# Activation stores in larger pieces and a new order on the DMA queues: two PEER layers on one Trainium2 core

## The chip, the cores and the metric

The kernel runs on one core of a Trainium2 chip. The metric is the device time of one execution in microseconds (us). A core has five engines with an instruction stream each: TensorE (PE; its weight loads are shown as PEld), VectorE (DVE), ScalarE (ACT), GpSimd (POOL) and SyncE (SP). SP computes nothing here; it issues nearly all DMA transfers, one after the other, in the order in which they stand in its stream. POOL issues the indirect transfers (gathers). All transfers are carried out by the same 16 DMA engines.

## The reference: what is computed

The input is 256 tokens of width 1024. Two layers follow each other: an attention mixer (latent attention in layer 0, sparse attention with top-64 key selection in layer 1), each followed by a layer norm, a PEER mixer and another layer norm. The change lies in the PEER mixer, which both layers have:

```
q = (xt @ w_q).reshape(T, PEER_HEADS, 2, PEER_QDIM // 2)
s1, s2 = q[:, :, 0] · sub_keys[0], q[:, :, 1] · sub_keys[1]      # 128 keys each
v1, i1 = top_k(s1, 16);  v2, i2 = top_k(s2, 16)
best, pos = top_k(v1[..., :, None] + v2[..., None, :], 16)       # of 256 pairs
expert = (i1 * 128 + i2)[pos];  gate = softmax(best)
a  = einsum('td,ted->te', x, w_down[expert])                     # T x (8 heads x 16)
y  = einsum('te,ted->td', gelu(a) * gate, w_up[expert])
```

There are 16384 experts. Each token uses 128 of them.

## The kernel before, in words

**PEER as dense work.** Instead of gathering 128 rows per token from `w_down`, the kernel multiplies all 16384 rows with all 256 tokens. The experts stand in 128 blocks of 128. In the down stage (`for b0 in range(0, NKEYS, 2)`, L1573), a step takes two blocks: each is loaded from HBM as a 128x1024 tile `raw` (512 KB, SP, L212), split into a high and a low 16-bit half (`hi` on ACT at L152, `lo` on DVE at L161), and multiplied in 24 matmuls of 128x256 (`d`, `proj`). The result goes through Gelu on ACT (L1584 or L1586) into `A`, an array of 128 blocks x 256 tokens in on-chip memory, and is multiplied there by the gates (DVE, L1418 and L1587). The gates come as one-hot products `G` on PE, in groups of four tokens (`place`, L1400): 64 groups in all, up to two in each step of the second half of the down stage, so tokens get final in their order, and the last four are final only after the last group.

**The up stage.** `A` is then multiplied by `w_up`. The first 20 expert blocks (DENSE = 20) are used as they are: their `raw` tiles are again loaded by SP at L212. For the other 108 blocks only experts that some token uses are wanted. So their rows of `w_up` are copied, HBM to HBM, into a table (`table<-in_up`, L217, 512 KB each), the activations of `A` are stored behind them in the same table rows (`table<-arena`, L1542), and POOL gathers rows of the table, weights and activations together, by a list that DVE computes at that time (`lists`, L1421). The up stage runs over 124 items (`ITEMS`): 20 dense ones first, then the gathered ones. An item for all tokens is 12 matmuls of 128x512 (`y`). Dense items take their left operand from `A` in pairs (`cut`, L1553: `xh` on ACT, `xl` on DVE; the first pair in a spare buffer).

**What sets the order.** `Stream` (L164 on) hands blocks out. When block i is taken, blocks up to i + 3 are split (AHEAD) and blocks up to five further are loaded (DMA_AHEAD); a block's number in the stream is part of its name (`raw172`). There are six `raw` buffers, so the load of block n waits until DVE has made `lo` of block n - 6. The copies of `w_up` rows are tied to loads by `copies(li)` (L411): a table of stream positions; behind the load at such a position up to two copies are issued. In layer 0 the blocks of the down stage are 39 to 166, the dense up blocks 167 to 186, the first gathered item 187.

The stores are issued by `store(part, upto)` (L1534): one store moves four blocks of `A` for the tokens of one part, so that each of its 512 rows is as long as the part has tokens. `PARTS` (L74) cuts the tokens at 128, 192 and 224: four parts, 27 stores each in a layer. In a step of the down stage each part whose tokens are final is offered up to two stores (part 0) or three (others), L1599 to L1603. The rest follow in the first items of the up stage (L1657 to L1659). At item 12 (HEAD - 8) all stores must have been issued, and the look-ahead is raised to eight, which brings the first gathers.

The instructions of an engine run strictly in the order of its stream. That order is not that of the program text: a scheduler that models times lays it out, so a changed transfer can move ACT or DVE instructions far from it.

The lines that matter most around the stores:

```
PARTS = (0, 128), (128, 192), (192, 224), (224, 256)
...
                    if 4 * groups >= upto:
                        for _ in range(2 if part == 0 else 3):
                            store(part, b0)
```

Of the kernel before, what the change touches and what calls it, by code (L numbers as in the profile page):

```python
# [68 lines left out]
DENSE, HEAD = 20, 20  # L69
RARE = P - DENSE  # L70
JB, JO, TB, ROWTAIL = 32, 24, 16, 32
BOTHS = JB + TB
WIDE = D + T
PARTS = (0, 128), (128, 192), (192, 224), (224, 256)  # L74
FETCHED, DEEP = 9, 8
LISTED = BOTHS + 2 * JO
END = 6
# [257 lines left out]
def tile_trunk(ctx: ExitStack, tc: tile.TileContext, ins, out: bass.AP, short, shared):  # L335
# [75 lines left out]
    def copies(li):  # L411

        down = len(ws.blocks) - NKEYS
        first, few = ((12, 24), (down - 44, 46))[li]
        for n in range(RARE + 1):
            i = first + (down - first) * n // few if n < few else down + 108 * (n - few) // (RARE + 1 - few)
            ws.copied.setdefault(i, []).append((table[li][n * P : (n + 1) * P, :D], ins["up"][li][(DENSE + n) % NKEYS]))

    def add_up(li):
# [13 lines left out]
    ws = Stream(nc, raws, rings, half, split, spare16)  # L433
# [758 lines left out]
    def peer(li):  # L1192
        last = li == DEPTH - 1
# [337 lines left out]

        stored = [DENSE] * len(PARTS)

        def store(part, upto):  # L1534
# [3 lines left out]
            if b0 < b1 <= upto:  # L1538
                ts = slice(*PARTS[part])
                cols = slice(D + ts.start, D + ts.stop)  # L1540
# [32 lines left out]
        for b0 in range(0, NKEYS, 2):  # L1573
            p = ps(f"d{b0}")
            pv = p.rearrange("p (j t) -> p j t", t=T)
            chosen = ready
            for j in range(2):
                proj(pv[:, j, :], ws.get())
                ready = ready or spend(PACE)
            if b0 == 0:  # L1580
                chains["pe"] = None
            t0 = 4 * groups
            if t0 < T:
                nc.scalar.activation(A[:, b0 : b0 + 2, t0:], pv[:, :, t0:], AF.Gelu, scale=1.0 / unit)  # L1584
            if t0 > 0:
                nc.scalar.activation(pv[:, :, :t0], pv[:, :, :t0], AF.Gelu, scale=1.0 / unit)  # L1586
                dve(lambda: nc.vector.tensor_tensor(A[:, b0 : b0 + 2, :t0], A[:, b0 : b0 + 2, :t0], pv[:, :, :t0],  # L1587
                                                    op=ALU.mult))
            while groups < prepared:
                place(groups, b0 + 2)  # L1590
                groups += 1
            if chosen:
                left = max(1, (NKEYS - (END if short else 4) - b0) // 2)
                want = min(64 - groups, -(-(64 - groups) // left))
                assert want <= 3, b0
                for _ in range(min(want, 1 + groups)):
                    prepare(prepared, nc.gpsimd if want == 1 else nc.vector)
                    prepared += 1
            if short:  # L1599
                for part, (_, upto) in enumerate(PARTS):  # L1600
                    if 4 * groups >= upto:
                        for _ in range(2 if part == 0 else 3):
                            store(part, b0)  # L1603
                if groups == 64:
                    if listing[0] is None:
                        chains["dve"] = None
                        cut(0)
                        listing[0] = lists()
                    if b0 < NKEYS - 2:
                        list_on(3)  # L1610
# [34 lines left out]
        if short:  # L1645
            for i, (_, _, tiles) in enumerate(ITEMS):
                if i + 2 in PAIRED:
                    cut(PAIRED.index(i + 2))
                if i < len(ITEMS) - STAGGER:
                    blk = ws.get()  # L1650
                    rows(y4, activations(i), blk, i == 0, False, tiles)
                list_on(1)
                if i == TAIL_READY:
                    assert next(listing[0], 0) == 0
                    chains.pop("dve")
                    chains.pop("pe")
                if i < HEAD - 8:  # L1657
                    for part in range(len(PARTS)):
                        store(part, NKEYS)  # L1659
                    store(part, NKEYS)  # L1660
                if i == HEAD - 8:
                    assert stored == [NKEYS] * len(PARTS) and not ws.due, stored
                    ws.pieces = 2
                    ws.DMA_AHEAD = DEEP
                if i == len(ITEMS) - 9:
                    ws.pieces = 1
                    ws.DMA_AHEAD = Stream.DMA_AHEAD
                if i == len(ITEMS) // 2:
                    middle_loads()
            items = [(activations(i), ITEMS[i][2]) for i in range(len(ITEMS) - STAGGER, len(ITEMS))]  # L1670
        else:
            for k in range(NKEYS - STAGGER):
                rows(y4, operand(k), ws.get(), k == 0, False)
                if k == 64:
                    middle_loads()
            items = [(operand(k), (0, 1)) for k in range(NKEYS - STAGGER, NKEYS)]
# [9 lines left out]
    for c in range(0, NC, 4):  # L1686
        last = nc.sync.dma_start(xt[:, c : c + 4, :], ins["xT"][c // 4])
# [154 lines left out]
```

## Time and profile before

| | |
|---|---|
| median of 3 runs | 1579.84 us (1578.42 to 1582.33) |
| the profiled execution | 1576.3 us, its span 1574.4 us |
| PE busy | 1544.1 us, 98% of the span |
| DVE, ACT, POOL busy | 1362.9, 1081.9, 386.0 us |
| DMA | 491.11 MB, 312 GB/s on average |
| `table<-in_up` copies | 218 of 512 KB |
| `table<-arena` stores | 54 of 256 KB, 56 of 128 KB, 108 of 64 KB |

Reading it: times inside the profile count from the start of the span. Matmuls are pipelined, so the rows show how long one takes from its start to its end, while the next may begin earlier; work per time is read from starts (the chain of waits gives such pieces). The view by windows gives, for stretches of the span, the busy time of PE, PEld, DVE, ACT and POOL in this order with instruction counts, then the granted PE clock, the DMA engines' busy share and the GB/s moved. A row of the timeline gives start, duration, engine, line, operation and tile, and in square brackets how long the engine had been idle and what ended that. "SPq" is SP's queue: an issue of a DMA, which includes waits for the transfer's preconditions.

### The profile page before, as it was taken

To read this page: it belongs to the slowest core of one execution; us is meant where nothing else is said; L and a number is where in the kernel's file an instruction comes from. 1 tells how busy PE (TensorE), PEld (TensorE's weight loads), DVE (VectorE), ACT (ScalarE), POOL (GpSimd) and SP (SyncE) were. 2 spreads that over 40 slices of the span, in tenths; PEclk is the share of its full clock that TensorE was granted. 3 is DMA by queue.
4 is the path that set the end of the run, shared out by engine and by line. 5 is a ranking of instruction groups with operands and counts; after the bars stand their busy time and mean duration, and the time that the engine had idled before them with its cause. 6 is when DMAs were issued, how large, how long until landed. Compare 5 with 4: busy or idle time off the path is not lost.

```text
span 1574.4 us, 33700 instructions
## 1 busy us (share of the span) xinstructions
PE 1544.1 (98%) x12275; PEld 1136.9 (72%) x12275; DVE 1362.9 (87%) x3823; ACT 1081.9 (69%) x1968; POOL 386.0 (25%) x330
## 2 busy tenths in 40 slices
PE   9999999999999999999999999999999999999996
PEld 7769888899999444444578598878899996444443
DVE  8689999999998779788788789989999996798886
ACT  7766566698887457676577766655988884567763
POOL 2002244300000046554022111344000000366550
PEclk9999999999999999999999999999999999999998
DMA  9898899998989999998499978889878899899992
GB/s 367 333 332 322 308 335 355 368 334 301 301 284 235 238 396 346 360 370 326 166 418 378 366 289 285 317 285 319 318 272 277 290 248 215 323 319 370 388 334 88
DMA packets 235760, 491.11 MB, mean 312 GB/s; under 512 B 99904, under 2 KB 128832, under 8 KB 235584
## 3 DMA queue, kind: packets, MB, share of 16 engines
q1 hardware_dynamic: 206496, 358.31, 65.7%
q0 software_dynamic: 28800, 130.04, 22.1%
q8 instruction: 98, 1.61, 0.4%
q14 instruction: 78, 0.64, 0.1%
q10 hardware_dynamic: 288, 0.52, 0.1%
HBM read 456.03 MB, written 147.06 MB: 383 GB/s over the span
## 4 chain that ended last, share of the span: by engine, by line
PE 82%; DVE 9%; DMA 3%; issue 2%; ACT 2%; SPq 1%; POOL 0%; DVEq 0%; POOLq 0%; ACTq 0%
PE y L477 32%; PE d L477 30%; PE pq L477 4%; DVE lo L161 4%; PE G L477 4%; PE q L477 3%; DMA raw<-in_down 2%; PE v L477 2%; PE seen L477 2%; ACT hi L152 1%; SPq L1542 1%; PE qw L477 1%; PE ps L477 1%; PE h L477 1%; DVE arena L1311 1%
## 5 line engine op out<-in xcount | busy, mean ns | idle before, releaser
L477 PE MATMUL d<-xh,lo 128*128 128x256 f16 x2048 | 558.3, 273 | 3.6 <-DVE lo L161 3.4
L477 PE MATMUL d<-xh,hi 128*128 128x256 f16 x2048 | 558.2, 273 | 1.8 <-ACT hi L152 1.8
L477 PE MATMUL d<-xl,hi 128*128 128x256 f16 x2048 | 558.2, 273 | 0.0
L477 PEld LDWEIGHTS <-hi 128*128 128x128 f16 x5016 | 488.5, 98 | 59.3 <-ACT hi L152 2.1
L161 DVE SCALAR_TENSOR_TENSOR lo<-raw,hi 128x1024 f16<-128x1024 f32 (+1 forms) x363 | 455.0, 1261 | 52.4 <-ACT hi L152 49.7
L152 ACT ACTIVATE hi<-raw 128x1024 f16<-128x1024 f32 (+1 forms) x355 | 368.1, 1048 | 171.5 <-PE d L477 63.5
L208 POOL DMA_INDIRECT arena<-table,up_at x160 | 174.9, 1093 | 668.6 <-DMA raw<-in_up 511.0
L477 PEld LDWEIGHTS <-xh 128*128 128x128 f16 x1712 | 166.6, 98 | 199.0 <-ACT xh L152 3.0
L161 DVE SCALAR_TENSOR_TENSOR lo<-arena,hi 128x512 f16<-128x512 f32 (+1 forms) x382 | 259.2, 715 | 45.2 <-ACT hi L152 44.5
L477 PEld LDWEIGHTS <-lo 128*128 128x128 f16 x2508 | 245.7, 98 | 35.2 <-DVE lo L161 6.3
L477 PE MATMUL y<-hi,xl 128*128 128x512 f16 x784 | 236.5, 380 | 6.6 <-DVE xl L161 6.6
L477 PE MATMUL y<-lo,xh 128*128 128x512 f16 x784 | 236.5, 380 | 0.0
L477 PE MATMUL y<-hi,xh 128*128 128x512 f16 x784 | 236.1, 380 | 0.0
L152 ACT ACTIVATE hi<-arena 128x1024 f16<-128x1024 f32 x200 | 209.1, 1052 | 14.3 <-PE y L477 3.9
L1397 ACT ACTIVATE gate<-hot,rest 128x128 f16<-128x128 f16 x512 | 168.5, 406 | 15.9 <-DVE hot L1389 14.0
L152 ACT ACTIVATE xh<-arena 128x256 f16<-128x256 f32 (+1 forms) x214 | 86.7, 407 | 116.8 <-PE y L477 74.9
L477 PEld LDWEIGHTS <-xl 128*128 128x128 f16 x856 | 83.6, 98 | 108.4 <-DVE xl L161 8.7
L262 POOL TENSOR_TENSOR lo<-raw,hi 128x1024 f16<-128x1024 f32 x26 | 58.9, 2264 | 193.0 <-ACT hi L260 138.8
L1389 DVE TENSOR_TENSOR hot<-iota,place 128x1024 f16<-128x1024 f16 x128 | 88.0, 689 | 15.7 <-PE G L477 15.4
L161 DVE SCALAR_TENSOR_TENSOR xl<-arena,xh 128x256 f16<-128x256 f32 (+2 forms) x216 | 89.8, 419 | 8.7 <-ACT xh L152 8.3
L477 PE MATMUL G<-gate,hot 128*128 128x128 f16 x1024 | 92.3, 219 | 1.3 <-DVE arena L1418 1.0
L1307 POOL TENSOR_TENSOR arena<-arena 128x800 f32<-128x800 f16 x32 | 73.3, 2290 | 73.1 <-DVE arena L1304 62.6
(270 smaller groups left out, 1862.1 us busy)
## 6 DMA issues: line engine op xcount, KB each, us to landing
raw<-in_down SPq DMA_DIRECT2D x256, 512.0 KB
table<-in_up SPq DMA_DIRECT2D x218, 512.0 KB
raw<-in_up SPq DMA_DIRECT2D x40, 512.0 KB
table<-arena SPq DMA_DIRECT2D x54, 256.0 KB
raw<-in_peer_q SPq DMA_DIRECT2D x24, 512.0 KB
raw<-in_dsa_qk SPq DMA_DIRECT2D x16, 512.0 KB
table<-arena SPq DMA_DIRECT2D x56, 128.0 KB
table<-arena SPq DMA_DIRECT2D x108, 64.0 KB
```

Of the source, the lines that this page charges most:

```text
L152: return nc.scalar.copy(o, src) if unit == 1.0 else nc.scalar.mul(o, src, unit)
L161: return nc.vector.scalar_tensor_tensor(o, src, unit, hi, op0=ALU.mult, op1=ALU.subtract, accum_out=total)
L208: self.fetched = self.nc.gpsimd.indirect_dma_start(t, None, table, bass.IndirectOffsetOnAxis(ap=at, axis=0)).ins
L262: nc.gpsimd.tensor_tensor(lo, raw, hi if short else hi.bitcast(F32), op=ALU.subtract)
L477: return pe(lambda: nc.tensor.matmul(o, l, r, start=start, stop=stop, skip_group_check=True))
L1307: nc.gpsimd.tensor_tensor(o.rearrange("p k c -> p c k"), same, cell[t][:, h, :, None].to_broadcast([P, CELLS, TOPK]), op=ALU.mult)
L1311: dve(lambda: nc.vector.tensor_reduce(exp_[t][:, h - 1, :], held, axis=AX.X, op=ALU.add))
L1389: nc.vector.tensor_tensor(hot, iota4[:, None].to_broadcast([P, 2, P, 4]), place16[:, :, None, four].to_broadcast([P, 2, P, 4]), op=ALU.is_ ...
L1397: nc.scalar.mul(gate[:, 1, j, :], hot[:, 1, :, j], rest[:, t : t + 1])
L1542: nc.sync.dma_start(rows_of, A[:, b0:b1, ts])
```

## The change

Five things are edited, in both layers alike.

1. `PARTS` has three parts; the last is tokens 192 to 255. Its 27 stores of 128 KB replace 54 of 64 KB.
2. Part 1 is now offered two stores in a step (three before), the last part three.
3. The stores of the up stage may run to item 13, and the first gather is requested two items later (HEAD - 6 in place of HEAD - 8).
4. From item 6 until then, the look-ahead of loads is three blocks in place of five.
5. `copies` spreads the 109 copies of a layer over three stretches of stream positions. Layer 0: 32 before the down stage (24 before), 38 over its first 64 loads, 39 over the next 36. Layer 1: 46 before it (as before), 32 over its first 64 loads, 31 over the next 36. Before, the rest (85 and 63) were spread evenly over the first 108 loads.

```diff
-PARTS = (0, 128), (128, 192), (192, 224), (224, 256)
+PARTS = (0, 128), (128, 192), (192, 256)
...
-        first, few = ((12, 24), (down - 44, 46))[li]
-        for n in range(RARE + 1):
-            i = first + (down - first) * n // few if n < few else down + 108 * (n - few) // (RARE + 1 - few)
+        spans = (12, down, 32) if li == 0 else (down - 44, down, 46), (down, down + 64, 38 - 6 * li), (down + 64, down + 100, 0)
+        at = [first + (last - first) * n // many for first, last, many in spans[:2] for n in range(many)]
+        first, last, _ = spans[2]
+        left = RARE + 1 - len(at)
+        at += [first + (last - first) * n // left for n in range(left)]
+        for n, i in enumerate(at):
             ws.copied.setdefault(i, []).append((table[li][n * P : (n + 1) * P, :D], ins["up"][li][(DENSE + n) % NKEYS]))
...
-                        for _ in range(2 if part == 0 else 3):
+                        for _ in range(3 if part == len(PARTS) - 1 else 2):
                             store(part, b0)
...
-                if i < HEAD - 8:
+                if i == HEAD - 14:
+                    ws.DMA_AHEAD = Stream.DMA_AHEAD - 2
+                if i < HEAD - 6:
                     for part in range(len(PARTS)):
                         store(part, NKEYS)
                     store(part, NKEYS)
-                if i == HEAD - 8:
+                if i == HEAD - 6:
                     assert stored == [NKEYS] * len(PARTS) and not ws.due, stored
```

What this does to the instruction streams is seen at three places. In the rows below, `raw167` to `raw178` are loads of dense up blocks of layer 0, `table0<-arena` are stores, and the last number of a store is its tokens; line numbers of the changed kernel are three higher from L420 on.

SP, from the end of the down stage into the up stage of layer 0, before:

```order
L212 DMA raw169_7455<-in_up 128x1024
L1542 DMA table0_119<-arena_65 128x4x32 x3
L212 DMA raw170_7485<-in_up 128x1024
L1542 DMA table0_119<-arena_65 128x4x32 x4
L1542 DMA table0_119<-arena_65 128x4x128
L1542 DMA table0_119<-arena_65 128x4x64
L1542 DMA table0_119<-arena_65 128x4x32 x3
L212 DMA raw171_7571<-in_up 128x1024
L1542 DMA table0_119<-arena_65 128x4x128
L1542 DMA table0_119<-arena_65 128x4x64
L1542 DMA table0_119<-arena_65 128x4x32 x10
L212 DMA raw172_7601<-in_up 128x1024
```

and now, in the same place:

```order
L212 DMA raw169_7435<-in_up 128x1024
L212 DMA raw170_7465<-in_up 128x1024
L1545 DMA table0_119<-arena_65 128x4x128
L1545 DMA table0_119<-arena_65 128x4x64
L212 DMA raw171_7549<-in_up 128x1024
L1545 DMA table0_119<-arena_65 128x4x128
L1545 DMA table0_119<-arena_65 128x4x64 x11
L212 DMA raw172_7579<-in_up 128x1024
L1545 DMA table0_119<-arena_65 128x4x64
L212 DMA raw173_7624<-in_up 128x1024
L1545 DMA table0_119<-arena_65 128x4x64 x7
L212 DMA raw174_7654<-in_up 128x1024
```

Between raw169 and raw171 stood 12 stores and now stand two; the 12 between raw171 and raw172 remain, 10 of them now of 64 tokens, which need the last group of gates.

ACT, at the first items of the up stage of layer 0 (`d126` is the last step of the down stage, `hi172` the split of the sixth dense up block), before:

```order
L1586 ACTIVATE d124_7566<-d124_7566 128x512
L152 ACTIVATE hi171_7743<-raw171_7571 128x1024
L152 ACTIVATE xh_100<-arena_65 128x512 x3
L152 ACTIVATE hi172_7768<-raw172_7601 128x1024
L1586 ACTIVATE d126_7643<-d126_7643 128x512
L152 ACTIVATE xh_100<-arena_65 128x512
```

and now:

```order
L1589 ACTIVATE d124_7544<-d124_7544 128x512
L152 ACTIVATE hi171_7717<-raw171_7549 128x1024
L152 ACTIVATE xh_100<-arena_65 128x512 x3
L1589 ACTIVATE d126_7619<-d126_7619 128x512
L152 ACTIVATE xh_100<-arena_65 128x512
L152 ACTIVATE hi172_7742<-raw172_7579 128x1024
```

The split that needs raw172 stood ahead of the Gelu of d126 and now stands behind it. Layer 1 shows the same exchange with hi469.

ACT, where the attention of layer 0 begins (`kn`, `v` are results of its projections, `hi18` and `hi19` splits of weights that are used after the attention, L821 the exponentials), before:

```order
L509 ACTIVATE arena_65<-kn2_610 128x512
L152 ACTIVATE hi18_943<-raw18_566 128x1024
L509 ACTIVATE arena_65<-kn4_631 128x512
L509 ACTIVATE arena_65<-kn6_645 128x512
L152 ACTIVATE hi19_947<-raw19_615 128x1024
L821 ACTIVATE arena_65,m_675<-arena_65,m_675 128x128
L509 ACTIVATE arena_65<-v00_701 128x512
L509 ACTIVATE arena_65<-v01_702 128x512
L821 ACTIVATE arena_65,m_677<-arena_65,m_677 128x256
```

and now:

```order
L512 ACTIVATE arena_65<-kn6_647 128x512
L512 ACTIVATE arena_65<-v00_704 128x512
L512 ACTIVATE arena_65<-v01_705 128x512
L152 ACTIVATE hi18_947<-raw18_568 128x1024
L512 ACTIVATE arena_65<-v10_706 128x512
L512 ACTIVATE arena_65<-v11_707 128x512
L824 ACTIVATE arena_65,m_678<-arena_65,m_678 128x128
L824 ACTIVATE arena_65,m_680<-arena_65,m_680 128x256
L152 ACTIVATE hi19_951<-raw19_617 128x1024
```

hi18 and hi19 have moved later, hi19 behind the first two exponentials; the copies of `v` now all stand ahead of them. PE and DVE are reordered to match in this stage, with the same instructions.

## The prediction, as put on record

> **What bounds the kernel now.** First the page's span and busy times:
>
> ```profile
> span 1574.4 us, 33700 instructions
> PE 1544.1 (98%) x12275; PEld 1136.9 (72%) x12275; DVE 1362.9 (87%) x3823; ACT 1081.9 (69%) x1968; POOL 386.0 (25%) x330
> ```
>
> PE is the bound, and the change takes no matmul away. It can only win time in which PE waits, or in which its clock is low: 30 us of the span at the very most. So the second view is the windows, cut at the stages; the columns are busy PE, PEld, DVE, ACT, POOL, then PE clock, DMA share, GB/s:
>
> ```profile
> 45.00:65.00 20.00, 19.67 (x129) 17.34 (x127) 18.05 (x83) 19.47 (x58) 0.23 (x1) 1.00 1.03 415
> 139.00:306.00 167.00, 164.88 (x1501) 146.27 (x1499) 157.06 (x465) 98.86 (x127) 60.20 (x38) 1.00 0.93 336
> 306.00:504.00 198.00, 197.49 (x2190) 181.38 (x2191) 186.69 (x340) 170.02 (x439) 0.00 (x0) 1.00 0.89 300
> 504.00:531.00 27.00, 23.30 (x194) 17.73 (x193) 14.81 (x38) 11.79 (x19) 0.00 (x0) 0.99 0.96 201
> 531.00:767.00 236.00, 236.00 (x1147) 108.33 (x1146) 196.75 (x699) 151.23 (x216) 106.70 (x101) 0.99 0.90 328
> 935.00:1056.00 121.00, 117.70 (x1072) 104.34 (x1070) 111.25 (x383) 71.58 (x91) 39.54 (x30) 1.00 0.83 291
> 1302.00:1328.00 26.00, 23.14 (x194) 17.67 (x193) 14.65 (x37) 11.96 (x18) 0.00 (x0) 1.00 0.92 199
> ```
>
> PE idles where the down stage turns into the up stage (27.00 - 23.30 = 3.70 us in layer 0, 26.00 - 23.14 = 2.86 in layer 1) and in the first half of the down stages (2.12 and 3.30). The second half (0.51 in 198 us) and the up stage (none in 236) have no idle time to win. Third, whom PE waits for:
>
> ```profile
> PE y L477 <- DVE xl L161: 6.6, 2, 3.7
> PE d L477 <- DVE lo L161: 3.4, 5, 1.0
> PE d L477 <- ACT hi L152: 1.8, 1, 1.8
> ```
>
> The two longest waits are the two turns. The chain of waits shows what stands behind that of layer 0 (start, duration, what):
>
> ```profile
> 511.20 0.60 DVE arena L1418
> ...
> 523.32 3.93 DMA raw<-in_up
> ...
> 527.35 1.06 ACT hi L152
> 528.41 0.49 ACT d L1586
> ...
> 528.92 0.69 DVE arena L1587
> 529.61 0.62 DVE xl L161 x2
> ...
> 530.28 34.66 PE y L477 x152
> ```
>
> PE did not yet need the tile raw172 that was loaded at 523.32. It needed `xl`, which DVE could not make because it stood in the Gelu product of the last step (L1587), which waited for ACT's Gelu (L1586), which stood in ACT's stream behind the split of raw172. SP's timeline says why that load was late:
>
> ```profile
> 513.97 0.45 SPq L212 DMA_DIRECT2D raw<-in_up  x1
> 514.52 8.69 SPq L1542 DMA_DIRECT2D table<-arena  x12
> 523.32 0.45 SPq L212 DMA_DIRECT2D raw<-in_up  x1
> ```
>
> Twelve stores, 8.69 us, between two loads.
>
> **The change part by part: the turn.** Layer 1's chain and PE's own rows in layer 0 give the price:
>
> ```profile
> 1320.19 3.99 DMA raw<-in_up
> ...
> 1327.22 32.98 PE y L477 x152
> ```
>
> ```profile
> 520.38 0.59 PE L477 MATMUL y<-hi,spare 128*128 128x512 f16 x2
> ...
> 530.28 1.03 PE L477 MATMUL y<-hi,xl 128*128 128x512 f16 x2 [3.70 <-DVE xl L161]
> ```
>
> The same 152 matmuls take 34.66 us behind the wait of 3.70 and 32.98 behind that of 2.86: 1.68 more. The granted clock of that window tells where:
>
> ```profile
> 530.00:550.00 20.00, 19.72 (x84) 8.67 (x85) 18.45 (x59) 7.99 (x10) 2.07 (x1) 0.91 1.00 264
> ```
>
> 0.91 against 1.00 elsewhere: 9% of 20 us is 1.8 us, the same loss. So the turns cost 3.70 + 1.68 + 2.86 = 8.24 us.
>
> Does the change remove all of it? Two things are needed. First, the Gelu of d126 must not wait for raw172: in the new ACT stream it stands ahead of it, in both layers, so the wait as it was cannot recur. What is late next is raw172 itself, the sixth dense item. An item is 12 matmuls of 32.98 / 152 = 0.217 us, 2.60 us; from 520.38, item 5 begins at 520.38 + 5 x 2.60 = 533.4. Before that come the split on ACT (1.06, in the chain) and on DVE:
>
> ```profile
> L161 DVE SCALAR_TENSOR_TENSOR lo<-raw,hi 128x1024 f16<-128x1024 f32 (+1 forms) x363 | 455.0, 1261 | 52.4 <-ACT hi L152 49.7
> ```
>
> With 1.26 for it and 3.93 for the landing, raw172 must be issued by 533.4 - 1.06 - 1.26 - 3.93 = 527.1. Now SP issues raw171 without waiting for the many stores ahead of it, so it stands ready at the next twelve. Ten of these need the last gates (L1418, done at 511.20 + 0.60 = 511.80). From there SP has 527.1 - 511.8 = 15.3 us for 12 stores, 1.27 each. What stores cost, in SP's timeline (64 tokens in both rows):
>
> ```profile
> 461.39 5.75 SPq L1542 DMA_DIRECT2D table<-arena  x10
> ...
> 468.32 7.57 SPq L1542 DMA_DIRECT2D table<-arena  x7
> ```
>
> 0.58 and, behind two loads, 1.08 us each; the twelve above 0.72. None reaches 1.27. At 0.72 raw172 is issued at 520.5, 6.6 us early, at 1.08 at 524.8. After it stand seven stores to raw174 (needed two items later) and then one to four between loads, so the slack grows by 2.60 us an item, against at most 4 x 1.08 + 0.45. I take the whole 8.24; the bounds are 8.24 and, with raw172 late after all, about half (below).
>
> **Fewer stores.** 54 issues at 0.58 to 1.08 go from SP, 31 to 58 us, all in places where PE was not waiting but for the turns; beyond them 0. The bytes stay. Offering part 1 less often happens where PE idled 0.51 us in 198: 0.
>
> **First gather two items later, look-ahead three.** SP's stream has no store behind raw178 now, so the shorter look-ahead reorders nothing that stalls SP; loads then wait for the six buffers as before. The gathers:
>
> ```profile
> 547.93 2.09 POOL L208 DMA_INDIRECT arena<-table,up_at  x1 [255.07 <-DMA raw<-in_up]
> ```
>
> ```profile
> 566.18 0.31 ACT L152 ACTIVATE xh<-arena 128x128 f16<-128x128 f32 x1 [6.12 <-DMA arena<-table,up_at]
> ```
>
> POOL has nothing else to do and waits for the last store, so its gather comes when the stores have landed, not when it was requested; with the last store issued earlier it comes earlier. ACT waited 6.12 us for its first rows, and PE idled not at all in that stage: 0, with a rival below.
>
> **The copies.** Layer 0 gets 8 more before the down stage, 8 x 0.524 MB = 4.2 MB, at the 415 GB/s of the windows 10.1 us of DMA time. Free there:
>
> ```profile
> 70.00:80.00 10.00, 10.00 (x49) 4.66 (x49) 3.07 (x7) 4.11 (x5) 0.00 (x0) 1.00 0.14 54
> ...
> 110.00:120.00 10.00, 10.00 (x94) 9.14 (x93) 9.49 (x45) 5.74 (x8) 1.70 (x1) 1.00 0.68 249
> ```
>
> 8.6 and 3.2 us, 11.8: just enough. In the first half of the down stage copies fall from 85/108 = 0.79 to 38/64 = 0.59 per load (layer 1: 0.58 to 0.50). The loads in the chain of that stage, where DVE is busy 157 of 167 us, are such:
>
> ```profile
> 245.87 4.66 DMA raw<-in_down
> ```
>
> 4.66 us against 3.93 with no copies near. A buffer's round trip shortens by less than 0.73 us, and only some of the 2.12 + 3.30 us of idle time hangs on it: between 0 and 5.4, I take 1.1 (0.8 and 0.3), close to the lower end, since DVE stays full. In the last stretch there are 39 copies for 36 loads. A step's two blocks take 48 `d` and 24 gate matmuls; 2190 / 72 = 30.4 steps in 198 us are 6.51 us each, 3.26 a block. 75 transfers of 0.524 MB in 36 x 3.26 = 117 us are 335 GB/s. The stage ran at 300, but 415 stands in the row for 45 to 65 us, with copies: hidden.
>
> **The attention of layer 0.** ACT is full there (19.47 of 20.00 us). hi18 and hi19 (1.05 each) now stand within the critical work: up to +2.1. Against that other filling work moved later and PE has 0.33 us idle by the row: down to -1. I take +0.5.
>
> Sum: -8.24 - 1.1 + 0.5 = -8.8 us. The profiled execution would take 1576.3 - 8.8 = 1567.5. It lay 3.5 below the median of the runs, so for the median 1579.84 - 8.8 = **1571.0 us**. About 0.3%, 4.7 us, is what a measurement can tell from no change.
>
> **Rivals.** *The turn moves to the next load* (0.13). If stores of 256-byte rows cost 1.5 us each, raw172 is issued at 511.8 + 12 x 1.5 = 529.8, 2.7 after 527.1; PE waits 2.7 per layer, and by layer 1's row a wait this long costs no clock. For: SP's 1.08 behind loads. Against: 0.72 in the same place. Time: 1571.0 + 5.4 = 1576.4.
>
> *Early copies delay the loads of the first 139 us* (0.08). Four of the eight fall into a stretch where DMA is full (1.03): 5 us of delay. If buffers don't hide it, 1576.0; against it, the weights loaded there are used only after the attention.
>
> *Gathers become late* (0.05; slower). If the first gather did come with its request, at item 14 (520.4 + 14 x 2.60 = 556.8), it would land 566.18 - 547.93 = 18.3 later, at 575.1, and be split by 577.4, while PE, no longer delayed, needs item 20 at 572.4: 5.0 us, and 1.7 for the clock, in each layer. 1571.0 + 13.4 = 1584.4, over the time before; it decides if POOL starts after 572.4 - 2.3 - 18.3 = 551.8. Against: POOL's wait ended with a transfer.
>
> *The last copies fill the memory* (0.02; slower). The down stage would fall behind while they run. The 300 GB/s of 306 to 504 us might be all that copies and loads get: 39.3 MB would take 131 us, 14 over 117, of which the six buffers hide nearly all. [...]
>
> **How the numbers follow.** Forecast 0.72. Its own bounds are 1571.0 - 4.3 (all idle time of the down stages) = 1566.7 and 1571.0 + 2.7 = 1573.7; the two milder rivals reach 1576.4; runs scatter by about 2. I give 1567 to 1577. Faster by over 0.3% (below 1575.1): 0.70 of the forecast, a third of the milder rivals' 0.21, 0.77 together. Within 0.3%: 0.16. Slower: 0.07, the last two rivals.
>
> **What would show it.** Right: no idle time of PE over 0.5 us where `spare` is followed by `xl` in either layer; the clock at 1.00 after it; ACT's Gelu at L1589 close behind `xh` x3; raw172's load about 520; the first gather near 540. Wrong: PE waiting for `lo` of the sixth to eighth dense block; PE idle at the first gathered item; longer stretches from 0 to 139 us or in the second half of the down stage.

## The result, and the profile after

The changed kernel takes 1565.96 us (median of six runs) against 1577.9 us (six runs of before), a ratio of 0.9928 with a 95% interval of 0.9912 to 0.9945: 9 to 14 us faster. A second set of runs of the same kernel gave 0.9924 (0.9907 to 0.9941). Executions in a slower state (at most one in a set) are left out of all ratios and ranges. The forecast was 8.8 us, counted from a median of three runs of before, 1579.84 us, and the measured time lies 1 us below its range. As a sum this looks like a small miss, but that is luck: two errors of opposite sign partly cancel. The turns, with what follows them, were taken at 8.24 us and gave about 4.1; the copies, with the attention's new order, were taken at 0.6 us and gave about 7.1.

The page of the changed kernel:

```profile
span 1566.8 us, 33568 instructions
PE 1544.2 (99%) x12275; PEld 1136.4 (73%) x12275; DVE 1360.7 (87%) x3815; ACT 1080.4 (69%) x1968; POOL 390.9 (25%) x330
```

PE's busy time is the same (1544.1 before), so by these rows the span lost 7.6 us of PE's idle time. The windows of the same stages (columns as in the prediction; the cuts move with the stages):

```profile
139.00:303.00 164.00, 163.84 (x1501) 146.51 (x1499) 153.31 (x461) 100.67 (x127) 60.38 (x38) 1.00 0.87 305
306.00:500.00 194.00, 193.52 (x2148) 177.68 (x2145) 182.96 (x334) 166.03 (x428) 0.00 (x0) 1.00 0.91 314
500.00:528.00 28.00, 28.00 (x227) 20.53 (x225) 21.83 (x60) 13.52 (x25) 0.00 (x0) 1.00 0.72 189
528.00:560.00 32.00, 32.00 (x150) 14.48 (x149) 21.78 (x64) 14.99 (x20) 12.04 (x9) 1.00 1.05 379
560.00:575.00 15.00, 13.55 (x62) 5.95 (x61) 9.05 (x34) 9.32 (x13) 2.23 (x2) 1.00 0.86 324
929.00:1050.00 121.00, 118.76 (x1080) 104.89 (x1079) 113.29 (x392) 72.27 (x94) 38.66 (x30) 1.00 0.80 279
1294.00:1322.00 28.00, 28.00 (x222) 20.35 (x220) 22.17 (x60) 13.52 (x22) 0.00 (x0) 1.00 0.74 197
1355.00:1370.00 15.00, 13.55 (x62) 5.89 (x61) 10.37 (x39) 9.01 (x14) 2.69 (x3) 1.00 0.27 94
```

Read it stage by stage. Both turns (500 to 528, 1294 to 1322) have no idle time any more: 3.70 and 2.86 us are gone, and the clock behind them is 1.00. But 45 us behind each turn there is idle time that before did not have: 15.00 - 13.55 = 1.45 us, the same in both layers. And the first half of layer 0's down stage, where 2.12 us were idle, now idles 0.16; layer 1's 2.24 where it was 3.30.

The turn went as forecast. SP's timeline: twelve stores in 6.88 us (0.57 each), then raw172's load, at 515.13.

```profile
508.15 6.88 SPq L1545 DMA_DIRECT2D table<-arena  x12
515.13 0.65 SPq L212 DMA_DIRECT2D raw<-in_up  x1
```

ACT's timeline there has the Gelu of the last step (L1589) ahead of the split that waits for raw172 (the `hi` with 1.13 of idle time before it):

```profile
515.69 1.74 ACT L152 ACTIVATE xh<-arena 128x512 f16<-128x512 f32 x3
517.46 0.58 ACT L1589 ACTIVATE d<-d 128x512 f32<-128x512 f32 x1
517.95 0.62 ACT L152 ACTIVATE xh<-arena 128x512 f16<-128x512 f32 x1
519.70 1.06 ACT L152 ACTIVATE hi<-raw 128x1024 f16<-128x1024 f32 x1 [1.13 <-DMA raw<-in_up]
```

POOL's first gather starts 8 us earlier than before (547.93):

```profile
539.97 1.77 POOL L208 DMA_INDIRECT arena<-table,up_at  x1 [250.23 <-DMA raw<-in_up]
```

The new wait is seen in PE's timeline, and behind it in ACT's:

```profile
566.06 0.59 PE L480 MATMUL y<-hi,xl 128*128 128x512 f16 x2
567.72 0.59 PE L480 MATMUL y<-hi,xh 128*128 128x512 f16 x2 [1.07 <-ACT hi L152]
```

```profile
561.45 1.04 ACT L152 ACTIVATE hi<-raw 128x1024 f16<-128x1024 f32 x1
563.21 0.31 ACT L152 ACTIVATE xh<-arena 128x128 f16<-128x128 f32 x1 [0.72 <-DMA arena<-table,up_at]
566.31 0.42 ACT L152 ACTIVATE xh<-arena 128x256 f16<-128x256 f32 x1 [2.79 <-PE y L480]
566.63 1.04 ACT L152 ACTIVATE hi<-raw 128x1024 f16<-128x1024 f32 x1
```

Count items from 0. The `hi` at 566.63 is hi186, for item 19, the last dense one. In ACT's stream it stands behind the `xh` of item 26. The buffer of that `xh` is the one that item 18 reads, so ACT waited 2.79 us until PE had finished item 18, made the `xh`, and only then the operand that PE needed next. PE has to stand still for 0.42 + 1.04 us here, however early the loads are. In before hi186 stood three `xh` further forward, ahead of those of items 24 to 26. ACT took its instructions in the order of its stream although a later one could run: with these `xh` moved behind it (below), hi186 is done 5 us earlier.

### The profile page after: what moved, and what is told of

Read it like the earlier page. It is cut to its first block, busy times and chain, and to the rows that moved or that the text cites. A ratio compares the mean times of both kernels' runs of the same rounds, so it can differ in the third digit from the quotient of the medians.

```text
span 1566.8 us, 33568 instructions
## 1 busy us (share of the span) xinstructions
PE 1544.2 (99%) x12275; PEld 1136.4 (73%) x12275; DVE 1360.7 (87%) x3815; ACT 1080.4 (69%) x1968; POOL 390.9 (25%) x330
## 4 chain that ended last, share of the span: by engine, by line
PE 90%; DVE 6%; issue 2%; ACT 1%; DMA 0%; POOL 0%; DVEq 0%; POOLq 0%; ACTq 0%
PE d L480 36%; PE y L480 32%; PE pq L480 4%; PE G L480 4%; DVE lo L161 3%; PE q L480 3%; PE v L480 2%; PE seen L480 2%; PE qw L480 1%; PE s L480 1%; PE ps L480 1%; PE h L480 1%; PE qi L480 1%; DVE arena L1314 1%; PE o L480 1%
## 5 line engine op out<-in xcount | busy, mean ns | idle before, releaser
L208 POOL DMA_INDIRECT arena<-table,up_at x160 | 180.9, 1131 | 655.0 <-DMA raw<-in_up 499.7
L152 ACT ACTIVATE xh<-arena 128x256 f16<-128x256 f32 (+2 forms) x214 | 85.7, 406 | 112.3 <-PE y L480 76.4
L480 PEld LDWEIGHTS <-hot 128*128 128x128 f16 x1536 | 89.1, 113 | 2.5 <-issue 1.2
```

The source lines that it names most:

```text
L152: return nc.scalar.copy(o, src) if unit == 1.0 else nc.scalar.mul(o, src, unit)
L208: self.fetched = self.nc.gpsimd.indirect_dma_start(t, None, table, bass.IndirectOffsetOnAxis(ap=at, axis=0)).ins
L480: return pe(lambda: nc.tensor.matmul(o, l, r, start=start, stop=stop, skip_group_check=True))
```

## Which part of the change gives what: four runs

Ratios are turned into us with the median of before beside them, 1577 to 1580 us; line numbers in the kernels below differ by a few.

Two theories. *A: the turns give 8 us less what item 19 takes back, and the copies give more than the forecast's 0.6 us (1.1 of gain, 0.5 of loss in the attention).* *B: the two traces are typical, the forecast's terms are about right, and the rest is scatter.*

**The changed kernel again**, nothing altered.

> The changed kernel once more, nothing altered. Between the two profiled executions the span fell by 7.6 us (1574.4 to 1566.8), but the medians of six runs fell by 11.9 us (1577.9 to 1565.96), and the profiled execution of the changed kernel was, with 1568.7, among the slowest of its six. Theory 'the trace is at the slow end of its kernel': the ratio comes out at 0.991 to 0.9945 again, and a second trace shows the same two new waits at the 20th item of the up stage (1.45 us idle, 1.9 us by cadence, in each layer), since they follow from the order of ACT's stream. Rival 'the traces are typical': ratio 0.995 +- 0.001.

Ratio 0.9924. Its trace idles 1.45 us at item 19 in both layers again, and 1.22 and 0.93 us in the first halves (0.16 and 2.24 in the first trace). So the gain is 11 to 12 us, and what the first halves lose differs from one execution to the next.

**Stores alone**: `PARTS` and the offers as in the changed kernel (edits 1 and 2), everything else as before.

> Before with three parts of tokens and the new number of offers alone (edits 1 and 2); copies, look-ahead and the last store item as before. Its ACT stream has the Gelu of d126 ahead of hi172 and of hi469, and hi186 and hi483 behind two xh of gathered items, as in the changed kernel; its attention stages stand as before. Theory 'the turns give 8 us less what the 20th item takes back': no idle time at the two turns, 1.4 us idle at the 20th item in each layer, the first half of the down stages idle as before (2.1 and 3.3 us): 3 to 5 us faster, ratio 0.997 to 0.998. Rival 'the stores are all of it': 10 us or more, ratio 0.9935 or lower.

Ratio 0.9974 (0.9961 to 0.9987): about 4.1 us. Its windows of layer 0 (first half, turn, item 19):

```profile
139.00:308.00 169.00, 165.02 (x1498) 145.65 (x1495) 157.68 (x465) 98.91 (x127) 59.21 (x38) 1.00 0.93 333
505.00:533.00 28.00, 28.00 (x229) 20.59 (x227) 21.71 (x62) 13.53 (x24) 0.00 (x0) 1.00 0.73 195
565.00:580.00 15.00, 13.55 (x62) 5.90 (x61) 8.91 (x34) 9.25 (x13) 2.23 (x2) 1.00 0.82 306
```

The turn is free, item 19 costs the same 1.45, and the first half idles 3.98 us. The scalings and splits of that half stand in the order of before, so I take the 2.12 us of the first trace to be a mild execution.

**Copies alone**: the new places of the copies (edit 5), everything else as before.

> Before with the new places of the copies alone (edit 5). Both turns keep their waits (3.7 and 2.9 us idle), and the order of the attention of layer 0 changes as in the changed kernel. Theory 'copies between the loads of the down stage's first half cost more than the forecast's 1.1 us': PE's idle time there falls from 2.1 to 0.2 us in layer 0 and from 3.3 to 2.2 in layer 1, as in the trace of the changed kernel, 3 to 5 us in all: ratio 0.997 to 0.998. Rival, the forecast: 0.6 us in all, ratio 0.9990 to 1.0000.

Ratio 0.9955 (0.9937 to 0.9972): about 7.1 us, where the forecast had 0.6. Both turns still stall, and the first half has no idle time at all:

```profile
139.00:302.00 163.00, 163.00 (x1497) 146.10 (x1496) 154.60 (x459) 100.52 (x128) 59.36 (x38) 1.00 0.87 305
499.00:527.00 28.00, 24.10 (x197) 18.12 (x196) 15.58 (x42) 11.99 (x20) 0.00 (x0) 0.96 0.91 194
```

So theory A holds, as far as single traces and these intervals go. The two ratios multiply to 0.9929, the whole of the result. That leaves nothing for the edits 3 and 4 (first gather later, shorter look-ahead), as forecast. They were not run by themselves; in the instruction streams they change nothing but four splits `lo` that are no longer cut in halves.

**An order of two instructions**: before, but in each layer hi172 (hi469) held behind the Gelu of d126 on ACT. No DMA is altered.

```diff
-                nc.scalar.activation(pv[:, :, :t0], pv[:, :, :t0], AF.Gelu, scale=1.0 / unit)
+                ws.gelu = nc.scalar.activation(pv[:, :, :t0], pv[:, :, :t0], AF.Gelu, scale=1.0 / unit).ins
...
-        act(lambda: self.split.high(hi, self.tiles[i][:, :w], unit))
+        with ExitStack() as order:
+            if i in (172, 469):
+                order.enter_context(self.after(self.gelu))
+            act(lambda: self.split.high(hi, self.tiles[i][:, :w], unit))
```

> Before with nothing but the order of two ACT instructions exchanged in each layer: the split of raw172 (raw469) is held behind the Gelu of d126. Stores, copies, loads and PE's and SP's streams are as before, so twelve stores (8.7 us) still stand ahead of raw172's load. Theory 'the turn was lost by the order on ACT': the idle time of 3.7 and 2.9 us at the turns and the low clock behind it go; then the gathers' rows are the next that is late: hi185 stands behind an xh that waits for the first gather (landed 566.2 in the trace of before), and PE, 5.4 us earlier, needs it at 567.2: 1 to 2 us idle there in each layer. Sum 4 to 7 us faster, ratio 0.9955 to 0.9975. Rival 'the stores' time on SP is what counts': PE then waits for lo172 about as long as it did for xl, ratio 0.9985 or higher.

Ratio 0.9956 (0.9942 to 0.997): about 7 us, with all the stores of before in their old places. The turn and the stretch behind it:

```profile
505.00:533.00 28.00, 28.00 (x221) 20.33 (x219) 20.94 (x55) 12.36 (x20) 0.00 (x0) 1.00 0.93 195
533.00:565.00 32.00, 31.36 (x146) 13.85 (x144) 22.85 (x73) 14.20 (x17) 10.90 (x9) 1.00 1.01 330
```

So the stall at the turns came from the order on ACT. That the stores ran long ahead of raw172's load decides nothing once the Gelu does not stand behind it. The later wait that I expected, for hi185, did not come in layer 1; layer 0 idles 0.64 + 0.24 us there, but for `xl`.

## Why item 19 waits, and how the copies gain: four runs

**The 20th item**: the changed kernel, with the `xh` of items 25 and 26 held behind hi186 (hi483).

```diff
-        act(lambda: self.split.high(hi, self.tiles[i][:, :w], unit))
+        made = act(lambda: self.split.high(hi, self.tiles[i][:, :w], unit))
+        if i in (186, 483):
+            self.dense = made.ins
...
-            act(lambda: self.split.high(high, self.tiles[i][:, D : D + high.shape[1]], unit))
+            with ExitStack() as order:
+                if i in (192, 193, 489, 490):
+                    order.enter_context(self.after(self.dense))
+                act(lambda: self.split.high(high, self.tiles[i][:, D : D + high.shape[1]], unit))
```

> The changed kernel with one order on ACT altered in each layer: the xh of the 26th and 27th up item (numbers counted from 0: 25 and 26) are held behind hi186 (hi483), the split of the last dense block. SP, PE and POOL have the same streams as in the changed kernel. Theory 'the new wait at the 20th item comes from an xh that waits for PE to finish item 18, with hi186 behind it': the idle time of 1.45 us and the 2.7 us of lost cadence there go in both layers, about 5 us less than the changed kernel, ratio 0.9885 to 0.9905. Rival 'the 20th item is late because its load or the full DMA is late' (DMA share 1.05 there): the wait stays, now with the load or DVE's lo as the one that ends it, ratio 0.992 to 0.993 as the changed kernel.

Ratio 0.9894 (0.988 to 0.9908), about 5 us less than the changed kernel. ACT now makes hi185 and hi186 together, hi186 5 us earlier, and PE has no idle time there:

```profile
560.56 1.99 ACT L152 ACTIVATE hi<-raw 128x1024 f16<-128x1024 f32 x2
562.45 4.83 ACT L152 ACTIVATE hi<-arena 128x1024 f16<-128x1024 f32 x5
567.18 0.60 ACT L152 ACTIVATE xh<-arena 128x128 f16<-128x128 f32 x2
```

```profile
559.00:575.00 16.00, 16.00 (x76) 7.25 (x75) 13.16 (x48) 10.39 (x14) 4.08 (x4) 1.00 1.00 387
```

The 5 us are more than the 2.9 us that the two layers idled at item 19. In this trace the first halves idle 0 and 0.75 us, 1.4 to 1.6 us less than in the two traces of the changed kernel, so part of the difference may be scatter.

**New copies and exchanged Gelu**, the stores as before:

> Before with the new places of the copies (edit 5) and the exchange of Gelu and hi172 (hi469) on ACT, but with the stores in four parts, the offers, the look-ahead and the last store item as before. Theory 'the two gains lie in different places, and the stores as such are worth nothing': the gains of the two single runs add, 0.9956 x 0.9955 = 0.991, so 14 us, faster than the changed kernel, which loses 2.7 us per layer at the 20th item. Rival 'fewer stores are worth something by themselves': slower than the changed kernel, ratio 0.993 or higher.

Ratio 0.9897 (0.9883 to 0.9912): the gains add (0.991 expected). Without one store altered this is at least as fast as the changed kernel, by the ratios some 4 to 5 us faster, though the intervals touch.

**Fewer copies still in the first halves**: as the last run, but

```diff
-        spans = ..., (down, down + 64, 38 - 6 * li), (down + 64, down + 100, 0)
+        spans = ..., (down, down + 64, 25), (down + 64, down + 108, 0)
```

> The run with new copies and exchanged Gelu, but with 25 copies over the first 64 loads of the down stage in both layers (38 and 32 there), and the rest (52 and 38) over the next 44 loads. 0.39 copies per load in place of 0.59 and 0.50. Theory 'each copy between the loads of the first half costs PE time there, since a load lands later': PE's lost time in the first halves, some 4 us with 0.59 and 0.50 and 8 with the old 0.79 and 0.58, falls to about 1 to 2, another 2 us: ratio 0.989 to 0.990. Rival 'below 0.59 per load nothing hangs on the copies any more' or 'the second half is now overfull (52 copies and 44 loads)': equal to or slower than the run with 38 and 32, with idle time behind the first G.

Ratio 0.992 (0.9904 to 0.9937). The theory had it faster than the last run; by the ratios it is 3.6 us slower, with intervals that overlap. In layer 0 the theory of fewer copies fell. With 0.39 copies per load the loads of layer 0's first half (139 to 306 us) land sooner. The DMA issues (count, size, median us from issue to landing), first with the new copies alone, then in this run:

```profile
raw<-in_down SPq DMA_DIRECT2D x61, 512.0 KB, 5.0
```

```profile
raw<-in_down SPq DMA_DIRECT2D x60, 512.0 KB, 4.2
```

And yet the first half of layer 0 idles again:

```profile
139.00:306.00 167.00, 164.43 (x1502) 145.80 (x1500) 156.73 (x458) 98.68 (x127) 59.48 (x38) 1.00 0.75 262
532.00:564.00 32.00, 29.21 (x134) 12.75 (x133) 24.00 (x75) 15.47 (x18) 9.61 (x8) 1.00 1.00 314
```

The first half idles 2.57 us, with the DMA engines 75% busy. The 2.79 us in the up stage were not followed further.

**Without the eight early copies**: before with the new places, but in layer 0 `(12, down, 24)`, so that the eight go into the last stretch.

> Before with the new places of the copies, but in layer 0 only 24 copies ahead of the down stage as before; the other eight go into the last stretch (47 for 36 loads). The streams of PE, DVE and POOL are then exactly those of before, the attention's order too. Theory 'the gain comes from fewer copies between the loads of the first half': the first half of layer 0 loses under 1.5 us as in the run with all the new copies, and the time is 0.9955 to 0.997. Rival 'the early eight, or the attention's new order, are what counts': ratio 0.998 or more; rival 'the last copies fill the memory' (335 GB/s then 83 x 0.524 MB in 117 us, 371 GB/s): idle time of PE between the first G and the turn of layer 0.

Ratio 0.9983 (0.9969 to 0.9997), about 2.7 us in place of 7.1. The first half of layer 0 has exactly the copies of the run with all new places, between the same loads, and yet:

```profile
139.00:308.00 169.00, 165.58 (x1505) 146.22 (x1505) 158.05 (x467) 99.17 (x127) 58.40 (x38) 1.00 0.84 295
308.00:505.00 197.00, 196.52 (x2181) 180.45 (x2179) 185.95 (x339) 168.97 (x436) 0.00 (x0) 1.00 0.94 335
```

The first half idles 3.42 us. In the second half 47 copies among 36 loads do no harm (0.48 us idle, as before).

So in layer 0 the number of copies does not decide. The two kernels differ there in ACT's stream, at a place that the description of the change does not list. In this stage every fourth block but a few is split by way of POOL: ACT first scales `raw` in place (`raw<-raw`, L258), which needs that block's load. This is how it stood in before, and stands in the last two runs:

```
L258 ACTIVATE raw53_1949<-raw53_1949 128x1024
L152 ACTIVATE hi50_2025<-raw50_1837 128x1024
L1584 ACTIVATE arena_65<-d4_1870 128x512
```

ACT must wait for the load of block 53 before it may split block 50, whose load was issued three places earlier. With all the new places raw53 stands behind hi51, and the scalings of blocks 33 to 61 have all moved back in this way; those of raw81 and raw85 have not. (The run with 25 copies has the early eight too, yet there the scalings of blocks 53 to 61 stand as in before or earlier; so the early copies do not fix the order by themselves.) The waits of ACT from 139 to 306 us (us in total, times, longest), in before and with the new copies alone:

```profile
ACT raw L258 <- DMA raw<-in_down: 30.1, 5, 10.4
ACT hi L152 <- DMA raw<-in_down: 17.6, 13, 2.5
```

```profile
ACT raw L258 <- DMA raw<-in_down: 14.1, 3, 8.1
```

The longest wait of before in ACT's timeline:

```profile
239.82 1.06 ACT L258 ACTIVATE raw<-raw 128x1024 f32<-128x1024 f32 x1 [10.40 <-DMA raw<-in_down]
240.78 1.04 ACT L152 ACTIVATE hi<-raw 128x1024 f16<-128x1024 f32 x1
```

The scaling is that of raw81, the split behind it hi78. SP had issued the load of raw78 at 227.01, 13.8 us before that split:

```profile
227.01 0.33 SPq L212 DMA_DIRECT2D raw<-in_down  x1
```

It is the turn's mechanism a second time. In the changed kernel this last wait is still there, and the 1.22 us that its second trace idles in the first half lie just behind it (242 to 250 us).

Layer 1 is another matter. With the new places its scalings of raw349, raw353 and raw357 stand one split earlier than in before, not later, and yet its first half idles 0.75 to 2.24 us in six traces with the new places and 0.36 with 25 copies, against 3.30, 2.62 and 1.26 in three with the old places. Fewer copies may well gain something there, and the 2.7 us of the run without the early eight may come from it; no run separates this.

## The order alone: three runs

**Scaling held back**: before, with the scaling of every fourth block held behind the `hi` two blocks earlier, in the first half of both down stages. Twelve ACT instructions move (seven in layer 0, raw81's and raw85's among them, five in layer 1); SP, DVE, PE and POOL have the streams of before.

```diff
-            self.act(lambda: nc.scalar.mul(raw, raw, unit))
+            with ExitStack() as order:
+                if 48 < i < 98 or 345 < i < 395:
+                    order.enter_context(self.after(self.made[i - 2].ins))
+                self.act(lambda: nc.scalar.mul(raw, raw, unit))
```

> Before with one order on ACT altered in the first half of both down stages: every fourth block goes over POOL, and its scaling on ACT (raw<-raw) stood in before ahead of the splits hi of blocks that are loaded two and three places earlier; here it is held behind the hi of the block two places earlier, as the new copies leave it in layer 0. Streams of SP, DVE, PE and POOL, the copies and their places are those of before. Theory 'the copies gained by the order of ACT, not by there being fewer of them': PE's lost time in the first half of layer 0 falls from 3.5 to 6 us to under 1.5, in layer 1 from 2.5 to 5 to under 3; 4 to 6 us in all, ratio 0.996 to 0.9975. Rival 'the number of copies per load is what counts' (0.79 and 0.58 remain): ratio 0.9985 or more, the loss in layer 0 stays above 3 us.

Ratio 0.9964 (0.9953 to 0.9975), about 5.7 us. The waits of ACT over the same stretch, the landing of loads, then the windows of both first halves and of both turns:

```profile
ACT hi L152 <- DMA raw<-in_down: 19.5, 16, 2.2
...
ACT raw L262 <- DMA raw<-in_down: 7.5, 3, 3.9
```

```profile
raw<-in_down SPq DMA_DIRECT2D x62, 512.0 KB, 6.0
```

```profile
139.00:303.00 164.00, 164.00 (x1505) 147.00 (x1504) 159.17 (x467) 101.14 (x127) 59.24 (x38) 1.00 0.94 343
500.00:528.00 28.00, 24.78 (x211) 18.89 (x209) 15.94 (x41) 12.82 (x23) 0.00 (x0) 1.00 0.94 196
...
932.00:1050.00 118.00, 118.00 (x1083) 105.85 (x1082) 113.38 (x397) 74.03 (x94) 39.91 (x30) 1.00 0.87 306
1294.00:1320.00 26.00, 23.11 (x191) 17.37 (x190) 14.59 (x40) 11.95 (x18) 0.00 (x0) 1.00 0.92 200
1320.00:1350.00 30.00, 30.00 (x133) 13.27 (x132) 26.76 (x83) 14.41 (x17) 10.91 (x9) 0.94 1.00 328
```

No idle time in either first half, with the old 0.79 and 0.58 copies per load, the DMA engines 94% busy in layer 0, and loads that take 6.0 us to land. ACT's waits for loads at the scaling fell from 30.1 to 7.5 us. The turns stall as before. In layer 0 the order alone thus removes what the new places removed. Layer 1, whose first half idled 1.26 to 3.30 us in the kernels with its old order and places, has a share in the 5.7 us.

**Both orders, no DMA**: before with this order and the exchange of Gelu and split.

> Before with both orders on ACT altered (scaling of every fourth block held behind, Gelu of d126 ahead of hi172 and hi469), and not one DMA moved, resized or removed. Theory 'the whole change works through the order of ACT's stream': 7 us of the turns and 4 to 6 of the first halves add, ratio 0.991 to 0.9935, as fast as the changed kernel. Rival 'the DMA edits give some of it themselves': ratio 0.994 or more.

Ratio 0.9917 (0.9899 to 0.9936): by the intervals as fast as the changed kernel, with not a byte moved differently. The first halves idle 0.65 and 0 us, the turns 0. So the order alone can give as much as the change. That all of the change's gain comes in this way is not shown by it, as the next run tells.

**Both orders mended in the changed kernel**: the two `xh` behind hi186, and the scaling held back.

> The changed kernel with both orders on ACT mended: the xh of items 25 and 26 behind hi186 (hi483), and the scaling of every fourth block behind the hi two places earlier in both layers. The run with the first of these alone gave 0.9894. What is left to win is the loss in layer 1's first half (1.7 us in that trace) and in layer 0's where an execution still shows it (0.8 to 2.6 in two traces of the changed kernel). Theory: 0.987 to 0.9895, 0 to 3 us less than that run. Rival 'layer 1's loss is DVE's own work and not ACT's order': no difference, 0.9885 to 0.9905.

Ratio 0.9893 (0.9872 to 0.9914); its four runs take 1558.65 to 1560.67 us. Its trace is the shortest of all, with a span of 1556.9 us, and PE idles 0 us in both turns, at item 19 and in layer 0's first half, 0.15 in layer 1's. Against the run with the first of these orders alone (0.9894) no difference can be told from the times. Against the run with both orders and no DMA edit (1562.96 to 1565.68 us in its five runs) it is 3.6 us faster by the medians, and no run of the one reaches the other. Some 2 us of this are seen in the windows: that run still idles 0.65 us in layer 0's first half and 0.87 at item 19, and 0.7 more in the attention of layer 0 (next section). The rest was not traced. So the DMA edits, and the orders that come with them, do give a little beyond these two orders.

The recorded expectations also speak of lost time, counted from the starts of the matmuls; it is larger than the idle time that the windows show. PE's idle time in us, from the windows of each trace (`item 19` is the stretch of some 30 to 60 us behind a turn):

| kernel | first half, turn, item 19: layer 0 | the same: layer 1 | ratio |
|---|---|---|---|
| before | 2.12, 3.70, 0 | 3.30, 2.86, 0 | 1 |
| the changed kernel, twice | 0.16 and 1.22, 0, 1.45 | 2.24 and 0.93, 0, 1.45 | 0.9928, 0.9924 |
| stores alone | 3.98, 0, 1.45 | 2.62, 0, 1.45 | 0.9974 |
| copies alone | 0, 3.90, 0 | 1.53, 2.26, 0 | 0.9955 |
| copies without the early eight | 3.42, 3.16, 0 | 1.05, 2.26, 0 | 0.9983 |
| Gelu exchanged | 3.09, 0, 0.88 | 1.26, 0, 0 | 0.9956 |
| Gelu exchanged, new copies | 0, 0, 0.92 | 1.43, 0, 0 | 0.9897 |
| the same, 25 copies per first half | 2.57, 0, 3.48 | 0.36, 0, 0 | 0.992 |
| scaling held back | 0, 3.22, 0 | 0, 2.89, 0 | 0.9964 |
| both orders, no DMA | 0.65, 0, 0.87 | 0, 0, 0 | 0.9917 |
| changed, `xh` mended | 0, 0, 0 | 0.75, 0, 0 | 0.9894 |
| changed, both orders mended | 0, 0, 0 | 0.15, 0, 0 | 0.9893 |

## Why the prediction was wrong, step by step

- *PE is the bound, and only its waits and its clock can be won.* Right: PE's busy time is the same to 0.1 us.
- *The turns.* The mechanism was right, and its price nearly so: the wait went in both layers, the low clock behind it too, and the exchange of two instructions by itself gave 7 of the 8.24 us. The step that failed is "what is late next is raw172 itself". The prediction sought the next late thing among the loads and on SP alone, and found 6.6 us of slack there, which was real (raw172 was forecast for about 520 and issued at 515.13). The next late thing was in ACT's stream 14 items further on: an `xh` that waits for PE with hi186 behind it, 1.45 us of idle time in each layer. So the term measured 4.1 us (2.1 to 6.2) by the run with the stores alone.
- *Fewer stores: nothing by themselves.* Right within the noise: with the new copies and no stall at the turns, the stores of before gave 0.9897, and the new stores, once item 19 is mended, 0.9894.
- *First gather and look-ahead: 0.* Right, as far as the other two parts leave nothing over; it was not run by itself.
- *The copies: 1.1 us.* The step that failed is that the gain hangs on "a buffer's round trip" and that it stays small "since DVE stays full". The prediction's own line of `lo` has 52.4 us of idle time on DVE, 49.7 of them for `hi` on ACT; and ACT was waiting, 30.1 us in the first half of layer 0, for loads of later blocks than the one that it had to split next. With the eight early copies among the new places, the scalings of eight blocks stand further back in ACT's stream. With them the new copies gave 7.1 us, without them 2.7, and such an order alone, with the old copies, 5.7 over both layers. This is the step that took the time below the range: the prediction compared the new order with the old at the turns and in the attention, and left out ACT's order in the down stage. (Whether the early copies act in a second way beside it was not separated; 0.7 us of it is the attention, below.)
- *The attention of layer 0: +0.5.* Wrong in sign, and small. Before and after, the windows behind it:

```profile
65.00:139.00 74.00, 73.12 (x521) 52.35 (x520) 54.18 (x171) 43.84 (x63) 7.73 (x5) 1.00 0.81 299
```

```profile
65.00:139.00 74.00, 73.81 (x527) 52.86 (x526) 54.53 (x179) 44.08 (x63) 8.47 (x5) 1.00 0.95 354
```

  PE idles 0.19 us there in place of 0.88, and 0.30 in place of 0.33 in the full stretch from 45 to 65 us. The 0.19 stands in every trace with the early copies, the 0.88 in every trace without them, so this is no scatter. The early copies delayed nothing, though DMA is 95% busy there now.
- *The rivals.* None came: the turn did not move to raw172, the early copies delayed nothing, the gathers are early, and the last copies do no harm: the second half of layer 0 moves 314 GB/s in the changed kernel and 335 with 47 copies in its stretch, and idles 0.48 us in both. No run shows them making the kernel slower; the 300 GB/s that the rival reckons with give 14 us, by its own words nearly all hidden.
- *The range.* Its lower end took all the idle time that one trace shows in the first halves, 5.4 us, as the most that could be won. Three kernels with the order of before in layer 0, or nearly so (stores alone, Gelu exchanged, copies without the early eight) idled 3.98, 3.09 and 3.42 us there, the trace of before 2.12. The two profiled executions also lie at opposite sides: 1576.3 is under the median of before, 1568.7 above that of the changed kernel, so the traces show 7.6 of the 11.9 us.

What stays open is why the scheduler moved the scaling when the copies moved, and what fewer copies are worth in layer 1. That the scaling moved in layer 0, and what such an order is worth by itself, was shown.

## What to carry to other kernels

When streams are laid out by a scheduler, compare the order on every engine over the whole program, not only near the edit: moving eight transfers to the first 139 us was worth some 4 us, most of it between 139 and 306 us, where the scalings had changed places on ACT. In a stream that runs in its order, as ACT's did in these traces (10.40 us of waiting ahead of hi78, 2.79 ahead of hi186), look for an instruction that waits for a late thing (a load just issued, a buffer that PE still reads) and stands ahead of one whose inputs have long been there; when a stall is removed, look for the next such pair downstream, since PE then arrives earlier. And take the idle time of one trace as one sample: nearly the same order lost 2.1 to 4.0 us in the same stage.

## What was not expected of the hardware

Whether PE's clock falls after a stall is not decided by the stall's length alone. At the turns, idle times of 3.70, 3.90, 3.16 and 2.89 us were followed by a granted clock of 0.93 to 0.95 over the next 30 us; 3.22, 2.86, 2.26 and 2.26 us were not (1.00). The run with the scaling held back shows both, 3.22 us without and 2.89 us with the low clock (1320 to 1350 us, 0.94). In its chain the same 152 matmuls take 1.69 us more behind the shorter stall:

```profile
526.66 32.98 PE y L481 x152
...
1318.60 34.67 PE y L481 x152
```

So the forecast's "a wait this long costs no clock" rested on one row and does not hold in general, and the 1.68 us that it counted for the clock of layer 0 is one sample too. What decides it beside the length, no run shows.
